# Sixteen gate chunks of a streaming-encoder layer computed as eight 2x2 block products of seven

## The chip, the cores and the metric

The kernel runs on one core of a Trainium2 chip. The metric is the device time of one execution in microseconds (us), the median of several runs. Engines: TensorE (PE in the profile, its weight loads PEld), VectorE (DVE), ScalarE (ACT), GpSimd (POOL) and SyncE (SP), whose queue issues most DMAs. Each runs its own instructions in order and waits on semaphores for the others.

## The reference

One layer of a residual encoder on x of 1024 tokens by 1024 channels, float32. Of its three sub-layers only the first is touched:

```python
h = rms_norm(x, norm_mix_pre)
q, k, v, u, gate_logits = split(h @ w_in)          # 512 columns each, gate_logits 2048
gate_attn, gate_ssm = split(sigmoid(gate_logits + b_gate))
merged = gate_attn * (stick_breaking_attention(q, k, v) @ w_branch_attn) \
       + gate_ssm * (s5_branch(u) @ w_branch_ssm)
x = x + rms_norm(merged @ w_out, norm_mix_post)
```

Cross-attention into 256 memory tokens and a gated MLP with a causal convolution follow. The change concerns the 2048 columns of gate_logits, 1024 tokens by 1024 by 2048, which before are computed as sixteen chunks of 128 columns.

## The kernel before

**Products in three parts.** A float32 operand is split into a high part (a cast to fp32r on ScalarE) and a low part (the difference, on VectorE). `mm3` (L140) makes each product of three matmuls: high by high, high by low, low by high. A step of TensorE is one `mm3` on a 128x128 stationary and a 128x512 moving tile, planned at STEP = 0.70 us.

**The order.** Up to the branches' merge, order is written by a planner. `at(t, go)` (L227) puts a piece of work at a planned time, and `all_events` issues everything sorted by that time, so planned times set only the order in each engine's queue. On the chip an instruction starts when it is first in its queue and its tiles are ready.

**hT.** The normalised input, x times the gain, transposed, lies in SBUF as high and low parts (`hT`, L333, four tiles of 16 KB per partition in pool ha); the rate of each token (the root-mean-square factor) is applied after the products. v and u are projected first (`tokens`, L423), token blocks against w_in.

**Gate chunks.** `gate_job(gi)` (L283) makes a `Job` (L242): load 512 KB of weights (`load`), cast the high part (`high`, ScalarE), subtract for the low part (`low`, L257, VectorE), and for two halves of 512 tokens eight steps over k into a PSUM bank of tag f (two banks). Then ScalarE copies the bank to SBUF (L288) and a DMA stores it in g_d in DRAM. In all 16 chunks x 2 halves x 8 steps. The merge, far behind, loads g_d again (`gate_load`), scales by the token's rate and applies the sigmoid with the bias (`gate_sigmoid`, L1310).

**Where they run.** The gate steps fill TensorE in two stages. Chunks EARLY_SSM (seven) run beside the SSM branch: `fill_to` (L848) lays one step after the other between the planned instructions of eight SSM slots. A slot n is `flip_u` (transpose u), `states` (L727: matmuls, then VectorE rotates by cosT and sinT, scans, and rotates back into rc, L741 to L753), `outputs` (L759: matmuls with Tt and with rc, then GELU on ScalarE). Slots are SLOT = 12.2 us apart, outputs 9.5 us after states. Between them VectorE prepares what later slots need: `tables` (L641, cosT and sinT of two slots), `operators` (L660, W) and `readout` (L672, F1). After two slots `flip_y` transposes y; when the last is done, `y_high` and `y_low` split it and the GLU follows: four `glu_job`s of eight steps on yh and yl. The other nine chunks, EARLY_ATT, run beside the attention, with the q and k projections of the four head pairs (`qk_job`), as a list `fills` into which the attention's groups (scores, transposes, weigh) are spread evenly: scores on TensorE, two sigmoids on ScalarE, a scan on VectorE (L1022), a product on GpSimd (L1028), transposes, high and low parts of the weights (L1049, L1054), and the product with v (L1067). Scores are laid some 20 us ahead of the transposes that use them.

**Buffers.** Raw weights sit in a ring of two (tag ws), parts in a ring of six (tag w), four tiles of 16 KB hold hT. The SSM stage has six PSUM banks of tag m.

The lines around the change:

## Time and profile before

| | before |
|---|---|
| runs | 1655.45, 1655.84, 1657.39 us |
| median | 1655.84 us |
| span of the profiled execution | 1653.9 us |
| HBM read, written in it | 204.0 MB, 67.4 MB |

The span runs from the first to the last instruction of one profiled execution. The page gives no separate time of that execution, so its span stands for it; the median of the runs is 1.9 us more. In the profile L12 is line 12 of the kernel, "out<-in" are names of tiles, and a row of the timeline is start, duration, engine, line, operation, tiles, shape and count, with idle time before it and what ended it in brackets. TensorE's durations overlap those of their neighbours, so its pace is the distance between two starts. The first 54 us project v, the next 47 u, the SSM stage runs to 218.4 us, the GLU to 240.8, the attention to 537.4, and memory keys and values, merge, cross-attention and MLP fill the rest.

### The profile page before, as it was taken

The numbers are of one execution on the slowest core, as the hardware profiler recorded it, in microseconds if no ns is written. First come the engines' busy times: TensorE is split into PE (matmuls) and PEld (weight loads), VectorE is DVE, ScalarE is ACT, GpSimd is POOL, SyncE is SP. The second block draws the span as 40 slices with busy tenths as digits, with TensorE's granted clock in tenths as the row PEclk, the third lists the DMA queues.
The fourth block names the chain that finished last, engine by engine and source line by source line (L and its number), as shares of the span: only waits on it lengthen the run. The fifth ranks groups of instructions, "written<-read, shape, count | busy, mean of one in ns | idle before, by whom it ended". The sixth has DMA issues, their size and how long they took to land.

```text
span 1653.9 us, 22415 instructions
## 1 busy us (share of the span) xinstructions
PE 1633.8 (99%) x8062; PEld 1379.8 (83%) x8062; DVE 1163.6 (70%) x1616; ACT 880.1 (53%) x1459; POOL 202.2 (12%) x296
## 2 busy tenths in 40 slices
PE   9999999999999999999999999999999999999998
PEld 7998887888888988888888888888888888888886
DVE  6778637776866687467655678888887788775473
ACT  5434346676766544344444556656565556654441
POOL 5000002333332000011000000111111111000010
PEclk9999999999999999999999999999999999999999
DMA  9412144232433954464423574677777676688672
GB/s 323 124 46 66 61 144 110 71 102 80 113 99 127 336 190 136 158 211 158 141 69 129 205 271 175 187 210 211 214 195 206 186 203 185 210 311 280 192 237 81
DMA packets 125439, 279.26 MB, mean 169 GB/s; under 512 B 23696, under 2 KB 28304, under 8 KB 125200
## 3 DMA queue, kind: packets, MB, share of 16 engines
q1 hardware_dynamic: 113664, 251.35, 46.1%
q0 software_dynamic: 9360, 18.09, 6.3%
q10 hardware_dynamic: 2304, 8.39, 1.3%
q8 instruction: 63, 1.03, 0.3%
q14 instruction: 48, 0.39, 0.1%
HBM read 203.98 MB, written 67.38 MB: 164 GB/s over the span
## 4 chain that ended last, share of the span: by engine, by line
PE 89%; DVE 6%; DMA 2%; ACT 2%; issue 1%; POOL 0%; SPq 0%; DVEq 0%; POOLq 0%; ACTq 0%
PE ps_p L1921 8%; PE ps_p L1919 8%; PE ps_p L1920 8%; PE ps_f L141 7%; PE ps_f L143 7%; PE ps_f L142 6%; PE ps_d L2190 4%; PE ps_d L2189 4%; PE ps_d L2191 4%; PE ps_m L141 3%; PE ps_m L143 3%; PE ps_m L142 3%; PE ps_o L1067 2%; PE ps_w L1042 2%; PE ps_z L141 1%; PE ps_z L142 1%
## 5 line engine op out<-in xcount | busy, mean ns | idle before, releaser
L141 PE MATMUL ps_f<-hT,wh 128*128 128x512 f32 x384 | 161.3, 420 | 0.0
L143 PE MATMUL ps_f<-hT,wl 128*128 128x512 f32 x384 | 150.8, 393 | 0.0
L142 PE MATMUL ps_f<-hT,wh 128*128 128x512 f32 x384 | 150.6, 392 | 0.0
L1920 PE MATMUL ps_p<-qS,bm 128*128 128x512 f32 (+2 forms) x368 | 140.4, 382 | 1.7 <-DVE qS L1744 1.7
L1919 PE MATMUL ps_p<-qS,bm 128*128 128x512 f32 (+2 forms) x368 | 140.5, 382 | 1.4 <-DVE uu L1937 0.9
L1921 PE MATMUL ps_p<-qS,bm 128*128 128x512 f32 (+2 forms) x368 | 140.5, 382 | 0.0
L147 DVE TENSOR_TENSOR dn<-raw,dn 128x1024 fp32r<-128x1024 f32 x77 | 93.4, 1223 | 63.0 <-ACT dn L146 59.2
L146 ACT CAST dn<-raw 128x1024 fp32r<-128x1024 f32 x77 | 80.5, 1054 | 87.2 <-PE ps_d L2191 36.4
L2189 PE MATMUL ps_d<-dn 128*128 128x512 f32 x308 | 119.8, 389 | 0.0
L2190 PE MATMUL ps_d<-dn 128*128 128x512 f32 x308 | 119.8, 389 | 0.0
L2191 PE MATMUL ps_d<-dn 128*128 128x512 f32 x308 | 119.8, 389 | 0.0
L1028 POOL TENSOR_TENSOR s<-s,s 128x127 f32<-128x127 f32 (+4 forms) x96 | 89.9, 937 | 223.8 <-DVE s L1022 178.6
L1921 PE MATMUL ps_p<-qA,bm 128*128 128x512 f32 (+2 forms) x272 | 105.1, 386 | 0.5 <-DVE bm L1850 0.5
L1919 PE MATMUL ps_p<-qA,bm 128*128 128x512 f32 (+2 forms) x272 | 105.3, 387 | 0.0
L1920 PE MATMUL ps_p<-qA,bm 128*128 128x512 f32 (+2 forms) x272 | 105.0, 386 | 0.0
L1932 ACT COPY uu<-ps_p 128x512 f32<-128x512 f32 (+2 forms) x90 | 51.5, 572 | 90.0 <-PE ps_p L1921 90.0
L1862 POOL DMA_DIRECT2D bm<-in_ffn_up_T x61 | 52.7, 864 | 356.6 <-ACT bm L1861 144.2
L143 PEld LDWEIGHTS ps_f<-hT,wl 128*128 128x128 f32 x384 | 72.1, 188 | 16.3
L1016 ACT ACTIVATE s<-ps_z,rates_x 128x128 f32<-128x128 f32 (+3 forms) x96 | 56.3, 587 | 54.0 <-PE ps_z L1005 47.8
L1919 PEld LDWEIGHTS ps_p<-qS,bm 128*128 128x128 f32 x368 | 69.2, 188 | 15.2 <-ACT uu L1932 2.2
L1920 PEld LDWEIGHTS ps_p<-qS,bm 128*128 128x128 f32 x368 | 69.2, 188 | 15.1 <-DVE qS L1744 2.0
L1921 PEld LDWEIGHTS ps_p<-qS,bm 128*128 128x128 f32 x368 | 69.3, 188 | 13.2
(544 smaller groups left out, 4462.2 us busy)
## 6 DMA issues: line engine op xcount, KB each, us to landing
raw<-sd SPq DMA_DIRECT2D x77, 256.0 KB, 3.5
bm<-in_ffn_up_T POOLq DMA_DIRECT2D x61, 256.0 KB, 5.4
ws<-in_w_in_T SPq DMA_DIRECT2D x24, 512.0 KB, 3.3
ws<-in_xa_wo_N SPq DMA_DIRECT2D x23, 512.0 KB, 4.3
wv<-in_ffn_up_T SPq DMA_DIRECT2D x22, 512.0 KB, 4.0
wg<-in_ffn_up_T SPq DMA_DIRECT2D x22, 512.0 KB, 3.8
dr<-in_ffn_down SPq DMA_DIRECT2D x22, 512.0 KB, 6.4
td<-st SPq DMA_DIRECT2D x44, 256.0 KB, 5.9
```

Source lines behind the costliest of these rows:

```text
L141: T.matmul(acc, sh, mh, start=first, stop=False)
L142: T.matmul(acc, sh, ml, start=False, stop=False)
L143: T.matmul(acc, sl, mh, start=False, stop=last)
L146: C.copy(dh, src)
L147: (lo or V).tensor_tensor(dl, src, f(dh), op=ALU.subtract)
L1028: G.tensor_tensor(s1[:, n0:e], s1[:, n0:e], s2[:, n0 + 1:e + 1], op=ALU.mult)
L1919: T.matmul(acc, bm[:, 0, ks], q[:, 0, k, cs], start=alone and k == 0, stop=False, skip_group_check=True)
L1920: T.matmul(acc, bm[:, 0, ks], q[:, 1, k, cs], start=False, stop=False, skip_group_check=True)
L1921: T.matmul(acc, bm[:, 1, ks], q[:, 0, k, cs], start=False, stop=k == 3, skip_group_check=True)
L2189: T.matmul(acc[i], v[:, 0, 0, sl], v[:, 0, 1], start=first, stop=False, skip_group_check=True)
L2190: T.matmul(acc[i], v[:, 0, 0, sl], v[:, 1, 1], start=False, stop=False, skip_group_check=True)
L2191: T.matmul(acc[i], v[:, 1, 0, sl], v[:, 0, 1], start=False, stop=last, skip_group_check=True)
```

## The change

Two neighbouring gate chunks m = 0, 1 (columns), two halves of the 1024 input channels and two halves of the tokens form a 2x2 by 2x2 block product, which is made of seven products instead of eight. The class `Product` is one of the seven for one of the eight pairs: four steps over k on a sum (or difference) of two weight blocks (`total`, or one block alone for products 2 and 5) and a moving tile. For products 3 and 4 the moving tile is a quarter of hT, for the others a quad: `quad(n, ...)` loads two quarters of x transposed (a new input x_Q), adds or subtracts them, multiplies by the gain, and splits the sum into high and low parts in the one tile of a new pool psl. That pool holds first the raw x tiles of the beginning, then quads 7, 6, 2, 5 and 1 in turn, each for all pairs that need it.

A product's result goes to one or two of the pair's four quadrants in g_d. The first that arrives is stored; a later one is added by a DMA that GpSimd issues with accumulate. Some pairs of products (4 and 7, and 3 and 6 for pairs 2 and 3) stay in one PSUM bank and leave it once. Where a product counts negative for one quadrant, the quadrant is kept negated, and the sigmoid takes a scale of -1 (`sign_of`).

Beside the SSM now run products 4 and 7 of all pairs, 3 of pairs 0 to 3 and 6 of all, 28 in all, with sums and low parts on GpSimd (`lower=G`). Beside the attention run 2, 5, 3 of pairs 4 to 7, and 1, with sums and low parts on VectorE. To make room in SBUF, tables are built in place, W and F1 have two buffers for three and four, q and k tiles share rings of three, s1 tiles are cut to size, oT has one buffer. `readout` 2 and 3 and `operators` 2 move from the u projection into the SSM slots, SLOT becomes 13.6 and outputs lie 10.5 us after states. One PSUM bank of tag m becomes tag g for products.

```diff
--- before.py
+++ after.py
+    FACTOR = {1: ((0, 0), (1, 1)), 2: ((0, 0),), 3: ((1, 0), (1, 1)), 4: ((0, 1), (0, 0)), 5: ((1, 1),),
+              6: ((0, 0), (1, 0)), 7: ((0, 1), (1, 1))}
+    QUAD = {1: ((0, 0), (1, 1)), 2: ((1, 0), (1, 1)), 5: ((0, 0), (0, 1)), 6: ((1, 0), (0, 0)), 7: ((0, 1), (1, 1))}
+    LESS = (3, 4, 6, 7)
+    GIVES = {1: {(0, 0): 1, (1, 1): 1}, 2: {(1, 0): 1, (1, 1): -1}, 3: {(0, 1): 1, (1, 1): 1}, 4: {(0, 0): 1, (1, 0): 1},
+             5: {(0, 0): -1, (0, 1): 1}, 6: {(1, 1): 1}, 7: {(0, 0): 1}}
+    CHAINED = {4: (0, 0), 3: (1, 1)}
+    def sign_of(gi, th):
+        return -1 if (gi % 2 if gi >= 8 else (gi + th) % 2) else 1
+    def first_in(pair, th, m):
+        if m == 0:
+            return (4,) if th else (7,)
+        if th == 0:
+            return (3,) if pair < 4 else (5,)
+        return (3,) if pair < 2 else (6,)
+    quads = {}
+    def quad(n, tag, t, parts=(0.0, 5.0), ahead=8.0):
+        (ta, ka), (tb, kb) = QUAD[n]
+        minus = n in LESS
+        rows, cs = {}, [slice(512 * j, 512 * j + 512) for j in range(2)]
+        def column(k, hh, j):
+            i = 4 * k + 2 * hh + j
+            return gcol[:, 0, i:i + 1]
+        def load(hh):
+            kw = {"bufs": WS} if tag == "ws" else {}
+            rows[hh] = [wpool.tile([P, 1024], F32, tag=tag, name="xq", **kw) for _ in range(2)]
+            for r, (th, kh) in zip(rows[hh], QUAD[n]):
+                dma(r, a["x_Q"][th, kh][:, hh * 1024:(hh + 1) * 1024])
+        def scaled(hh):
+            x = rows[hh][1]
+            for j in range(2):
+                C.activation(x[:, cs[j]], x[:, cs[j]], AF.Identity, bias=zcol, scale=column(kb, hh, j))
+        def total(hh):
+            xa, x = rows[hh]
+            if minus:
+                V.tensor_tensor(x, xa, x, op=ALU.subtract)
+                return
+            for j in range(2):
+                V.scalar_tensor_tensor(x[:, cs[j]], xa[:, cs[j]], column(ka, hh, j), x[:, cs[j]],
+                                       op0=ALU.mult, op1=ALU.add)
+        def high(hh):
+            if not hh:
+                quads[n] = psl.tile([P, 2, 4, 512], F32R, tag="slot", name="S")
+            for j in range(2):
+                dst, src = quads[n][:, 0, 2 * hh + j], rows[hh][1][:, cs[j]]
+                if minus:
+                    C.activation(dst, src, AF.Identity, bias=zcol, scale=column(ka, hh, j))
+                else:
+                    C.copy(dst, src)
+        def low(hh):
+            for j in range(2):
+                (h_, l_), src = (quads[n][:, m, 2 * hh + j] for m in range(2)), rows[hh][1][:, cs[j]]
+                if minus:
+                    V.scalar_tensor_tensor(l_, src, column(ka, hh, j), f(h_), op0=ALU.mult, op1=ALU.subtract)
+                else:
+                    V.tensor_tensor(l_, src, f(h_), op=ALU.subtract)
+        for hh, d in enumerate(parts):
+            at(t + d - ahead, lambda _, hh=hh: load(hh))
+            if not minus:
+                at(t + d - 2.2, lambda _, hh=hh: scaled(hh))
+            for go, dt_ in ((total, -1.3), (high, 0.0), (low, 1.3)):
+                at(t + d + dt_, lambda _, go=go, hh=hh: go(hh))
+    banks_of = {}
+    class Product:
+        home, tag = None, "f"
+        def __init__(self, pair, n, chain=None, lower=None):
+            self.i, self.n, self.chain, self.lower = pair, n, chain, lower or V
+            into = {}
+            for (th, m), sign in GIVES[n].items():
+                if chain == "begins" and (th, m) == CHAINED[n]:
+                    continue
+                into.setdefault(sign * sign_of(2 * pair + m, th), []).append((th, m, n not in first_in(pair, th, m)))
+            self.into = list(into.items())
+        def load(self, t):
+            self.ws = (wpool.tile([P, 1024], F32, tag="ws", name="ws", bufs=WS) if self.home is None else
+                       self.home.pool.tile([P, 1024], F32, tag="ws", name="ws", bufs=1))
+            for j, (m, k) in enumerate(FACTOR[self.n]):
+                dma(self.ws[:, j * 512:(j + 1) * 512], a["w_in_T"][8 + 2 * self.i + m][:, k * 512:(k + 1) * 512])
+        def total(self, t):
+            if len(FACTOR[self.n]) == 2:
+                self.lower.tensor_tensor(self.ws[:, :512], self.ws[:, :512], self.ws[:, 512:],
+                                op=ALU.subtract if self.n in (3, 4) else ALU.add)
+        def high(self, t):
+            self.bm = wpool.tile([P, 2, 512], F32R, tag="w", name="bm")
+            C.copy(self.bm[:, 0], self.ws[:, :512])
+        def low(self, t):
+            self.lower.tensor_tensor(self.bm[:, 1], self.ws[:, :512], f(self.bm[:, 0]), op=ALU.subtract)
+        def weights(self, t0, load=16.5, add=11.5, hi=9.0, lo=7.0):
+            for dt_, go in ((load, self.load), (add, self.total), (hi, self.high), (lo, self.low)):
+                at(t0 - dt_, go)
+        def step(self, t, k):
+            n = self.n
+            if n in QUAD:
+                mh, ml = (quads[n][:, j, k] for j in range(2))
+            else:
+                q, cols = (0, slice(0, 512)) if n == 3 else (1, slice(512, S))
+                mh, ml = (hT[j][q][:, k, cols] for j in range(2))
+            if k == 0:
+                self.acc = banks_of.pop(self.i) if self.chain == "ends" else ps(self.tag)
+                if self.chain == "begins":
+                    banks_of[self.i] = self.acc
+            wh, wl = (self.bm[:, j, k * P:(k + 1) * P] for j in range(2))
+            for j, (st, mv_) in enumerate(((wh, mh), (wh, ml), (wl, mh))):
+                T.matmul(self.acc, st, mv_, start=self.chain != "ends" and k == 0 and j == 0, stop=k == 3 and j == 2,
+                         skip_group_check=True)
+            if k == 3:
+                self.out(t + STEP + 0.2)
+        def out(self, t):
+            pool, tag, bufs = logs[-1]
+            def put(sign, places):
                 gt = pool.tile([P, 512], F32, tag=tag, name="glog", bufs=bufs)
-                C.copy(gt, acc)
-                dma(g_d[gi][:, sl], gt)
-
-            at(t, put)
-
-        return Job(a["w_in_T"][8 + gi], out)
+                if sign < 0:
+                    C.mul(gt, self.acc, -1.0)
+                else:
+                    C.copy(gt, self.acc)
+                for th, m, adds in places:
+                    dst = g_d[2 * self.i + m][:, th * 512:(th + 1) * 512]
+                    if adds:
+                        at(t + 1.5, lambda _, dst=dst: G.dma_start(dst, gt, accum_op=ALU.add))
+                    else:
+                        dma(dst, gt)
+            for x in self.into:
+                at(t, lambda _, x=x: put(*x))
...
-    ra.enter_context(banks(keep="f", m=(512, 6)))
+    ra.enter_context(banks(keep="f", m=(512, 5), g=(512, 1)))
...
-    logs.append((pa, "vt", 1))
+    logs.append((pa, "vt", 3))
+    xall = psl.tile([P, 4, KT, P], F32, tag="slot", name="xt")
...
-    SLOT = 12.2
+    SLOT = 13.6
...
-    at(u_begin + 33.2, lambda t: readout(t, 2))
-    at(u_begin + 35.4, lambda t: readout(t, 3))
-    at(u_begin + 37.6, lambda t: operators(t, 2))
+    quad(7, "ws", u_begin + 4.0, (0.0, 9.5), 7.0)
...
+    prods = []
+    for q in range(0, 8, 2):
+        prods += [Product(p, 4, "begins", lower=G) for p in (q, q + 1)]
+        prods += [Product(p, 7, "ends", lower=G) for p in (q, q + 1)]
+    prods += [Product(p, 3, lower=G) for p in (0, 1)]
+    prods += [Product(p, 3, "begins", lower=G) for p in (2, 3)]
+    prods += [Product(p, 6, "ends", lower=G) for p in (2, 3)]
+    prods += [Product(p, 6, lower=G) for p in (0, 1, 4, 5, 6, 7)]
+    tags = itertools.cycle("ffg")
+    for n, j in enumerate(prods):
+        j.home = open_t if n % 3 == 2 else None
+        j.tag = next(tags) if j.chain != "ends" else None
+        for k in range(4):
+            steady.append(lambda t, j=j, k=k: j.step(t, k))
+    first_of = {64 + 4 * n: j for n, j in enumerate(prods)}
...
+                if ns == 64 + 64:
+                    quad(6, "w", clock + 0.6, (0.0, 9.0))
...
-            plan(s0 + 9.5, 1.75, outputs, n)
+            plan(s0 + 10.5, 1.75, outputs, n)
...
-                if 1 <= n <= 4:
-                    at(s0 + 6.4, lambda t, n=n: readout(t, n + 3))
+                if n:
+                    at(s0 + 6.8, lambda t, n=n: readout(t, n + 1))
...
-            if n == 0:
-                at(s0 + 8.5, lambda t: operators(t, 3))
-            if n == 1:
-                at(s0 + 8.5, lambda t: tables(t, 3))
+            if n in (0, 2):
+                at(s0 + 8.5, lambda t, n=n: operators(t, 2 + n // 2))
+            if n in (1, 3):
+                at(s0 + 8.5, lambda t, n=n: tables(t, 2 + n // 2))
...
+    quad(2, "w", clock + 9.0, (0.0, 13.0), 8.0)
...
+    fills, phase = [], {n: [Product(p, n) for p in range(8)] for n in (2, 5, 1)}
+    phase[3] = [Product(p, 3) for p in (4, 5, 6, 7)]
+    def fill_pair(js, together=False):
+        seq = [(j, h) for h in range(2) for j in js] if together else [(j, h) for j in js for h in range(2)]
+        fills.extend((j, (h, k)) for j, h in seq for k in range(KT))
+    def fill_products(js):
+        fills.extend((j, (k,)) for j in js for k in range(4))
+    later = [[qk_job(pp, True), qk_job(pp, False)] for pp in range(1, 4)]
+    fill_pair(qk0, True)
+    fill_products(phase[2][:3])
+    fill_pair(later[0])
+    fill_products(phase[2][3:])
+    fill_pair(later[1])
+    fill_products(phase[5][:3])
+    fill_pair(later[2])
+    fill_products(phase[5][3:])
+    fill_products(phase[3])
+    fill_products(phase[1])
...
+        elif isinstance(job, Product):
+            job.weights(t0, 13.0, 7.0, *((2.6, 1.3) if job is phase[3][1] else (5.0, 3.8)))
+            t1 = ended[phase[2 if job.n == 5 else 5][-1]]
+            if job is phase[5][0]:
+                quad(5, "w", t1 + 11.0, (0.0, 17.5))
+            elif job is phase[1][0]:
+                quad(1, "w", t1 + 0.8, (0.0, 3.0), 11.5)
...
-        C.activation(gates[d, h][br], gates[d, h][br], AF.Sigmoid, bias=bgate[:, gi:gi + 1])
+        C.activation(gates[d, h][br], gates[d, h][br], AF.Sigmoid, bias=bgate[:, gi:gi + 1],
+                     scale=float(sign_of(gi, h)))
```

94 lines of the change are left out of this document (43 added, 51 removed).

## Prediction

> **What bounds the kernel now.** I read the page's first and fourth parts, then the windows by stage, then who TensorE waited for.
>
> ```profile
> span 1653.9 us, 22415 instructions
> PE 1633.8 (99%) x8062; PEld 1379.8 (83%) x8062; DVE 1163.6 (70%) x1616; ACT 880.1 (53%) x1459; POOL 202.2 (12%) x296
> PE 89%; DVE 6%; DMA 2%; ACT 2%; issue 1%; POOL 0%; SPq 0%; DVEq 0%; POOLq 0%; ACTq 0%
> ...
> 101.50:218.40 116.90, 116.23 (x676) 101.52 (x676) 87.76 (x147) 49.51 (x64) 1.19 (x9) 1.00 0.22 69
> 240.80:537.40 296.60, 294.89 (x1629) 250.75 (x1628) 209.66 (x279) 200.56 (x415) 92.19 (x159) 1.00 0.35 102
> 480.00:520.00 40.00, 40.00 (x223) 34.12 (x223) 26.47 (x36) 27.66 (x59) 14.12 (x24) 1.00 0.38 112
> ...
> PE ps_w L1042 <- DVE wtl L1054: 1.2, 2, 0.7
> PE ps_m L767 <- DVE rc L753: 0.7, 1, 0.7
> PE ps_o L1067 <- DVE wtl L1054: 0.6, 1, 0.6
> ```
>
> TensorE is the bound: busy 99% of the span, 89% of the chain of waits, clock 1.00. The window rows give us, then busy PE, PEld, DVE, ACT, POOL, the clock, the DMA share and GB/s. Gate work lies in two stages: beside the SSM (the first window, 112 steps of three matmuls) and beside the attention (the second, 144 gate steps and 128 of q and k). In both TensorE lacks under 2 us, and the three waits shown, 2.5 us together, are the ones on VectorE there. So a matmul taken out shortens the span by its pitch, as long as VectorE, with 71% of the attention and 75% of the SSM stage, keeps up. It has the next-fullest queue, and the change fills it.
>
> **What goes.** Sixteen chunks of two halves and eight k are 256 steps, 768 matmuls. Eight pairs, seven products, four k make 224 steps, 672 matmuls. The SSM stage keeps 112 steps, the attention goes from 272 to 240. Matmuls overlap, so their price is the pitch from start to start:
>
> ```profile
> 218.44 0.40 PE L141 MATMUL ps_f<-yh,wh 128*128 128x512 f32 x1
> 240.61 0.39 PE L143 MATMUL ps_f<-yh,wl 128*128 128x512 f32 x1
> 240.84 0.39 PE L141 MATMUL ps_f<-hT,wh 128*128 128x512 f32 x1
> 255.58 0.39 PE L143 MATMUL ps_f<-hT,wl 128*128 128x512 f32 x1
> ```
>
> Between the last two rows lie 65 pitches: 14.74/65 = 0.227 us on hT. 96 matmuls fewer are **-21.8 us**.
>
> **Slower operand.** The first two rows are the GLU: 95 pitches in 22.17 us, 0.2334. Its moving tiles lie in a late pool, hT's in an early one. The five quad sums go to a new pool behind hT, so 5 x 8 x 12 = 480 matmuls may run at the GLU's pitch: 480 x 0.0065 = **+3.1 us**, or 0 if they run like hT. I take 3.1: like yh they are new tiles outside hT's pool. The Trainium skill, SBUF — State Buffer, section Who interferes with whom, has TensorE waiting on nobody at SBUF; by that this term would be 0 and the sum 3.1 lower, but these rows show two pitches.
>
> **SSM stage.** Here each of eight slots is a chain: states on TensorE, rotation and scan on VectorE (L741 to L753), outputs on TensorE, which need rc. Slots come every 13.6 us by the new plan (12.2 before).
>
> ```profile
> 118.57 0.69 DVE L668 TENSOR_TENSOR W<-pr,X 128x512 f32<-128x512 f32 x1
> 120.50 0.69 DVE L668 TENSOR_TENSOR W<-pr,X 128x512 f32<-128x512 f32 x1
> ...
> 123.20 0.69 DVE L741 TENSOR_TENSOR bp<-ps_m,cosT 128x512 f32<-128x512 f32 x1 [0.69 <-PE ps_m L732]
> 125.33 0.69 DVE L744 TENSOR_TENSOR bp<-bp,bt 128x512 f32<-128x512 f32 x1
> ...
> 130.18 0.28 DVE L691 TENSOR_TENSOR ktt<-ps_m,dm 128x128 f32<-128x128 f32 x1
> ...
> 131.51 0.68 DVE L678 TENSOR_TENSOR F<-pr,Y 128x512 f32<-128x512 f32 x1
> ...
> 133.44 2.38 DVE L652 TENSOR_TENSOR x<-x,turns 128x8 f32<-128x8 f32 x7
> ...
> 137.72 0.68 DVE L741 TENSOR_TENSOR bp<-ps_m,cosT 128x512 f32<-128x512 f32 x1
> ```
>
> From start to start: a chain is 130.18 - 123.20 = 7.0 us (the first 2.1 of it read PSUM), a readout 1.9, a table 4.3, an operator pair of two halves 3.9. This slot was full already, its successor started late (no idle before 137.72), and TensorE paid the 0.7 us of L767. The change takes seven lows off VectorE and moves two readouts and one operator pair from the u projection into the slots. Slot 1 and slot 3 then hold 7.0 + 0.2 + 1.9 + 4.3 = 13.4 us, slot 2 12.8, slot 0 11.1, slots 4 and 5 with half of quad 6 each 7.0 + 1.9 + 2.4 = 11.3, slot 6 8.9. Alone this fits 13.6. But 28 products bring 56 sums of 512 columns to GpSimd (the halves' sum and the low part of each), by the plan's lead times 44 of them in slots 0 to 6, six in each, and the two engines shut each other out:
>
> ```profile
> 296.07 1.09 POOL L1028 TENSOR_TENSOR s<-s,s 128x511 f32<-128x511 f32 x1 [1.74 <-DVE s L1022]
> ...
> 296.21 2.03 DVE L259 TENSOR_TENSOR wl<-ws,wh 128x1024 fp32r<-128x1024 f32 x1 [0.29 <-ACT wh L255]
> ...
> 350.45 2.07 POOL L1028 TENSOR_TENSOR s<-s,s 128x511 f32<-128x511 f32 x1 [2.24 <-DVE s L1022]
> ...
> L259 DVE TENSOR_TENSOR wl<-ws,wh x28: 684/1218/2089, 100.8 to 514.8; 128x1024 fp32r<-128x1024 f32 x24, 128x512 fp32r<-128x512 f32 x4
> ```
>
> A VectorE low that meets a GpSimd product takes 2.03 us for a median of 1.22, 0.81 longer; a GpSimd product that comes second takes 2.07 for 1.09. One sum of six falls on the PSUM part of the chain, five meet the rest. In full that is 5 x 0.81 = 4.1 us a slot: slots 1, 2 and 3 come to 17.5, 16.9 and 17.5, slots 4 and 5 to 15.4, over 13.6 by 3.9 + 3.3 + 3.9 + 1.8 + 1.8 = 14.7 us. The outputs are planned 1 us later than before, and the chain, longer by two meetings, uses that up, so a late chain is a stall of TensorE; queued behind it are all further product steps. If half of the sums fall into gaps it is 2.0 a slot, and 1.8 + 1.2 + 1.8 = 4.8 us. I take the middle, **+10 us**, with 4.8 and 14.7 for the range.
>
> **The seam to the GLU.** By the plan's own times the last product step now lies before the outputs of slot 7; before, 14 steps came after them. They covered this:
>
> ```profile
> 206.40 0.39 PE L767 MATMUL ps_m<-F,rc 128*128 128x128 f32 x2
> 206.82 0.60 ACT L772 ACTIVATE y<-ps_m 128x512 f32<-128x512 f32 x1 [0.21 <-PE ps_m L767]
> 208.02 1.03 PE L783 MATMUL ps_m<-ident,y 128*128 128x128 f32 x8
> 212.52 1.22 DVE L916 TENSOR_TENSOR yl<-U,yh 128x1024 fp32r<-128x1024 f32 x1 [1.77 <-ACT yh L913]
> ```
>
> TensorE waits for the GELU (206.79 to 207.42, 0.7 us with its start), turns y until 1.03 us later, and the last yl is ready 213.74 - 209.05 = 4.7 us after that. The GLU can run three steps of 0.7 before it needs it: 2.6. Together **+3.3 us** (2.6 to 4).
>
> **Attention.** The lows stay on VectorE here.
>
> ```profile
> L1336 DVE TENSOR_TENSOR ml<-mm,mh 128x512 fp32r<-128x512 f32 x16 | 11.0, 689 | 4.8 <-ACT mh L1340 4.8
> L259 DVE TENSOR_TENSOR wl<-ws,wh 128x1024 fp32r<-128x1024 f32 x16 | 21.6, 1348 | 1.1 <-ACT wh L255 1.0
> L288 ACT COPY glog<-ps_f 128x512 f32<-128x512 f32 x18 | 10.6, 589 | 6.4 <-PE ps_f L143 5.9
> L1862 POOL DMA_DIRECT2D bm<-in_ffn_up_T x61 | 52.7, 864 | 356.6 <-ACT bm L1861 144.2 <-DVE uu L1937 136.1 <-DVE t L1826 35.4
> ```
>
> VectorE loses nine lows of 1.35 us (12) and gets 28 lows and 12 sums of half the width (40 x 0.69 = 28) and eight operations for each of quads 5 and 1 (11): 210 + 27 = 237 us in 297 - 22 = 275, 86% for 71%. ScalarE gets 28 copies out for 18, and 28 half casts for nine whole ones, and stays under 85%. GpSimd gets 52 accumulating DMAs at 0.86 us, 45 us on 92, and is half idle; each waits there for ScalarE's copy, and behind it are the products L1028, which run 20 us ahead of their transposes. On average nothing is full. The tightest stretch is product 3 of pairs 4 to 7 with quad 1: 16 steps. TensorE needs 0.68 us a step and its part of the attention, (296.6 - 272 x 0.68)/202 = 0.55, so 19.7 us. VectorE's attention work was 26.5 less two lows in 40 us, 0.6 of the time, and gets denser by a tenth: 12.7 us, with 8 x 0.69 and 5.5 for the quad 23.7, late by 4. Lows are planned 3.8 us ahead. I take **+3 us** for this and the q and k stretches, with 0 and 9 as ends (9 if both quads' 11 us are paid almost whole). The single quad slot is refilled while q and k or product 3 run on other tiles; I count it at nothing, and it is the cover for the quads' own 5.5 us each.
>
> **Smaller edits, queues and DMAs.**
>
> ```profile
> oa_d<-oT SPq DMA_DIRECT2D x16, 128.0 KB, 2.4
> ...
> SPq L289 <- ACT glog L288: 114.9, 26, 10.1
> ...
> 537.40:560.00 22.60, 22.60 (x188) 22.38 (x188) 15.85 (x20) 13.55 (x14) 1.05 (x1) 1.00 0.99 355
> ```
>
> The sign in the sigmoid, tables built in place, W and F with fewer buffers and the s1 tiles cut to size add no instruction, and their next user comes after the last reader in the plan: 0. One oT for two makes ScalarE's copy wait for two DMAs of 2.4 us at each head's end, some 3 us after they are issued: 0 to 1 us seven times on an engine that has 15% left, and I count 0. Loads and stores share SP's queue; it already waits up to 10 us for a copy without TensorE noticing, and the raw tiles (two, three beside the SSM) are free again about when the next load is due: 0. Traffic grows: weights 24 MB for 8, sums 54 x 0.25 MB read and written, quads 10 MB, some 45 MB over two stages with DMA shares of 0.22 and 0.35: hidden. Only the last product's two sums run into the memory stage, whose DMA share is 0.99 at 355 GB/s: 2 x 0.75 MB there are 4 us of DMA time. TensorE was busy throughout, so I take 0, with 4 as the end.
>
> **Sum: -21.8 + 3.1 + 10 + 3.3 + 3 = -2.4 us** on the profiled execution. Its page gives the span, 1653.9; the median of the timed runs is 1.9 higher, which I carry over: 1655.8 - 2.4 = 1653.4.
>
> **Rivals.** (A) GpSimd's sums mostly fall into gaps and the attention absorbs its load: -21.8 + 3.1 + 4.8 + 3.3 + 0 = -10.6, 1645; with hT's pitch for the quads 1642. For it: VectorE sits idle 29 us of the SSM stage. Against: those lie in the late slots. (B) Slower: the lock between VectorE and GpSimd is paid whole in slots 1 to 5 and TensorE waits at L767 for rc: -21.8 + 3.1 + 14.7 + 3.3 + 3 = +2.3, and with the attention's upper end +8.3: 1658 to 1664. It decides from 12.4 us of stalls upward. For it: both pairs of rows above show whole exclusion. The Trainium skill's SBUF page, same section, says just that: a VectorE instruction with two SBUF inputs and a GpSimd instruction that reads SBUF block each other for their whole length; the trace agrees (0.81 us a meeting), and by that rule B is the case. Against: a meeting costs only where VectorE has work waiting. The Trainium skill, TensorE: Matmul & The Clock Gate, Part 1, has the clock halved after an idle window of about 3.4 us and warm again after about as long a busy one; three stalls of 3.9 us would then add up to 3 x 1.7 = 5 us (an estimate from that page). Before shows a clock of 1.00 in every window, so no run here shows it yet. (C) The sums don't get shorter because the accumulating DMAs hold GpSimd and late weights stop TensorE in the attention: each of 24 products late by 1 us would be +24, 1675; the half-idle GpSimd speaks against it.
>
> **How the numbers follow.** My forecast (1648 to 1658) 0.42, A 0.28, B 0.26, C 0.04. A measurement can tell about 0.2%, 3.3 us, from no change. Faster by more than that, under 1652.5: A and 0.17 of the forecast, 0.45. Within: the rest of the forecast but a little, 0.22. Slower, over 1659.1: most of B, C and an edge, 0.33. The range leaves out the ends of A and C: 1641 to 1667.
>
> **What would show it.** Right: TensorE 96 matmuls fewer, each quad matmul at a pitch near 0.233; idle before the outputs' second matmul on rc of 5 to 15 us in slots 2 to 6; VectorE's two-input operations in the SSM stage at 1.5 us instead of 0.7 where a GpSimd sum runs; 3 us of idle at the GLU's first steps; VectorE at 85% in the attention. Wrong: no wait on rc, or waits of TensorE on bm (weights late), on the quad tile, or on ps_f's banks.

## The result and the profile after

The changed kernel takes 1713.82 us (median of four runs, 1710.07 to 1719.53) against 1656.47 beside it: 1.035 times as long, 95% interval 1.033 to 1.037. The forecast was 1653.4 with a range to 1667. The page of after, first and fourth parts:

```profile
span 1708.3 us, 22780 instructions
PE 1640.1 (96%) x7966; PEld 1375.5 (81%) x7966; DVE 1237.2 (72%) x1676; ACT 929.8 (54%) x1563; POOL 331.1 (19%) x406
PE 74%; DVE 9%; DMA 6%; ACT 4%; issue 4%; POOL 2%; SPq 1%; POOLq 0%; DVEq 0%; ACTq 0%
```

The 96 matmuls are gone (7966 for 8062), and yet TensorE is busy 6 us longer: some of its matmuls ran slower. It has also lost the chain of waits to others, 26% for 11%. The windows by stage, after, in the columns that the prediction explains, from the end of the u projection: SSM stage, GLU, attention (to the last product of transposed weights and v), rest.

```profile
103.70:251.80 148.10, 127.79 (x666) 107.85 (x664) 117.05 (x155) 67.29 (x103) 78.76 (x66) 0.91 0.53 167
251.80:277.10 25.30, 23.45 (x98) 17.68 (x96) 15.23 (x21) 17.62 (x24) 0.00 (x0) 1.00 0.55 199
277.10:593.20 316.10, 286.10 (x1533) 237.64 (x1532) 249.74 (x329) 220.39 (x464) 137.99 (x210) 0.98 0.71 180
593.20:1708.30 1115.10, 1102.31 (x5248) 921.96 (x5246) 785.09 (x1021) 571.19 (x895) 83.97 (x97) 1.00 0.61 191
```

Cut at the same places, before took 114.1, 22.2, 296.7 and 1116.6 (its u projection ends at 104.3 us; the prediction's first window began inside it). Its SSM stage and attention:

```profile
104.30:218.40 114.10, 113.43 (x665) 98.76 (x664) 87.26 (x146) 49.51 (x64) 1.19 (x9) 1.00 0.21 68
240.60:537.30 296.70, 294.99 (x1630) 250.84 (x1628) 209.66 (x279) 200.56 (x415) 92.19 (x159) 1.00 0.35 103
```

So the SSM stage lost 34.0 us, the GLU 3.1 and the attention 19.4, where 21.8 less was due; the rest is as it was. Who TensorE waited for in the SSM stage of after (us in total, times, longest):

```profile
PE ps_m L912 <- DVE rc L898: 6.0, 1, 6.0
PE ps_m L911 <- DMA ws<-in_w_in_T: 5.4, 1, 5.4
PE ps_m L876 <- ACT Ug L863: 3.4, 3, 2.6
PE ps_m L911 <- DMA Tt<-ktt: 2.4, 1, 2.4
```

L911 is the outputs' matmul on Tt, L912 the one on rc, L876 the states. L911 reads no weights, so I take its wait of 5.4 us, put down to a load of weights in the same DMA queue, as one for Tt too. With another 2.0 us of this kind, the waits for Tt come to 9.8. TensorE is idle 20.3 us of 148.1 there, and it waits for three things: VectorE's chain, the spread of Tt by DMA, and ScalarE's copy of Ug. The list of waits doesn't say which of them is the cause. In the attention it waits mostly for VectorE's and ScalarE's parts of the transposed weights:

```profile
PE ps_o L1221 <- DVE wtl L1208: 19.5, 17, 2.9
PE ps_o L1221 <- ACT wth L1203: 4.3, 4, 2.1
```

### The profile page after: what moved, and what is told of

Its sections match the earlier page's. It is cut to its first block, busy times and chain, and to the rows that moved or that the text cites. A ratio compares the mean times of both kernels' runs of the same rounds, so it can differ in the third digit from the quotient of the medians.

```text
span 1708.3 us, 22780 instructions
## 1 busy us (share of the span) xinstructions
PE 1640.1 (96%) x7966; PEld 1375.5 (81%) x7966; DVE 1237.2 (72%) x1676; ACT 929.8 (54%) x1563; POOL 331.1 (19%) x406
## 4 chain that ended last, share of the span: by engine, by line
PE 74%; DVE 9%; DMA 6%; ACT 4%; issue 4%; POOL 2%; SPq 1%; POOLq 0%; DVEq 0%; ACTq 0%
PE ps_p L2102 7%; PE ps_p L2100 7%; PE ps_p L2101 7%; PE ps_d L2370 4%; PE ps_d L2371 4%; PE ps_d L2372 4%; PE ps_f L141 3%; PE ps_f L142 3%; PE ps_f L411 3%; PE ps_f L143 3%; PE ps_m L141 2%; PE ps_m L143 2%; PE ps_m L142 2%; DMA ws<-in_w_in_T 2%; PE ps_z L141 1%
## 5 line engine op out<-in xcount | busy, mean ns | idle before, releaser
L1182 POOL TENSOR_TENSOR s<-s,s 128x127 f32<-128x127 f32 (+4 forms) x96 | 100.7, 1057 | 180.1 <-DVE s L1176 126.8
L411 PE MATMUL ps_f<-S,bm 128*128 128x512 f32 x420 | 121.9, 413 | 0.9 <-ACT glog L422 0.8
L2370 PE MATMUL ps_d<-dn 128*128 128x512 f32 x308 | 119.8, 389 | 0.0
L2371 PE MATMUL ps_d<-dn 128*128 128x512 f32 x308 | 119.8, 389 | 0.0
L2372 PE MATMUL ps_d<-dn 128*128 128x512 f32 x308 | 119.8, 389 | 0.0
L411 PEld LDWEIGHTS ps_f<-S,bm 128*128 128x128 f32 x420 | 75.6, 194 | 13.6 <-ACT glog L422 1.2
L210 POOL TENSOR_TENSOR rstd<-rstd,mhalf 128x1 f32<-128x1 f32 x24 | 21.7, 907 | 275.0 <-DVE rstd L208 233.8
L1176 DVE TENSOR_TENSOR_SCAN s<-s,begin 128x128 f32<-128x128 f32 (+1 forms) x64 | 63.7, 997 | 11.9 <-ACT s L1170 11.5
```

What stands on the lines that cost most here:

```text
L411: T.matmul(self.acc, st, mv_, start=self.chain != "ends" and k == 0 and j == 0, stop=k == 3 and j == 2, skip_group_check=True)
L1182: G.tensor_tensor(s1[:, n0:e], s1[:, n0:e], s2[:, n0 + 1:e + 1], op=ALU.mult)
L2370: T.matmul(acc[i], v[:, 0, 0, sl], v[:, 0, 1], start=first, stop=False, skip_group_check=True)
L2371: T.matmul(acc[i], v[:, 0, 0, sl], v[:, 1, 1], start=False, stop=False, skip_group_check=True)
L2372: T.matmul(acc[i], v[:, 1, 0, sl], v[:, 0, 1], start=False, stop=last, skip_group_check=True)
```

## The experiments

Lengths of the stages in the profiled executions, cut as above (us):

| kernel | SSM | attention | span |
|---|---|---|---|
| before | 114.1 | 296.7 | 1653.9 |
| the change | 148.1 | 316.1 | 1708.3 |
| e1 Tt spread by ScalarE's queue | 152.8 | 317.7 | 1717.1 |
| e2 no sums in the SSM stage | 126.5 | 316.1 | 1686.7 |
| e3 both | 124.6 | 315.7 | 1685.9 |
| e4 no sums of x (quads) | 141.1 | 305.7 | 1693.7 |
| e5 no sums, no quads anywhere | 117.4 | 311.1 | 1678.2 |
| e6 no accumulating DMAs | 145.5 | 293.9 | 1688.2 |
| e7 plain stores in their place | 147.9 | 299.5 | 1693.9 |
| e8 no sums of weights in the attention | 146.6 | 317.6 | 1710.4 |
| e9 GpSimd's sums over other tiles | 150.7 | 317.5 | 1714.5 |
| e10 two half output tiles | 147.5 | 317.1 | 1710.1 |
| e11 e5 without accumulating DMAs | 117.4 | 280.5 | 1646.9 |
| e12 powers of one column for these DMAs | 148.1 | 293.5 | 1687.8 |
| e13 e6 without quads | 142.2 | 285.2 | 1673.8 |
| e14 e6 and e8 | 148.4 | 285.7 | 1681.4 |
| e15 SSM sums on VectorE | 147.4 | 315.5 | 1711.9 |

Each experiment was timed once. Where one leaves a stage alone (but for the two accumulating DMAs that start in the SSM stage), the SSM stage repeats between 145.5 and 148.4 and the attention between 315.5 and 317.7, so 3 us in a stage are no reading.

### The SSM stage: queue, lock or room?

Three theories: TensorE's inputs are late because SyncE's queue stands still (Q), because VectorE and GpSimd shut each other out (L), or because VectorE is full anyway (F).

**e1** has the spread issued by ScalarE:

```diff
-            at(now + 1.3 * tau, lambda _, tau=tau: dma(Tt[...], ...))
+            at(now + 1.3 * tau, lambda _, tau=tau: C.dma_start(Tt[...], ...))
```

> The change in the SSM stage came out 33.9 us longer (114.1 to 148.0): waits of TensorE of about 20 us (9.8 of them outputs that wait for Tt, 6.0 for rc), the rest a lower clock after them. Here only the eight DMAs that spread Tt are issued by ScalarE instead of SyncE, whose queue holds weight loads that wait for GpSimd's low parts. Theory Q (the queue: Tt comes late because it stands behind weight loads): the three waits on Tt, 9.8 us, and the clock that they cost, some 7 us, go; the stage takes 129 to 133 us. Theory L (the lock of VectorE and GpSimd makes the chain late; Tt only happened to be the last of two late inputs): the outputs wait for rc instead, the stage stays above 142.

The stage got no shorter, 152.8. TensorE still waited for Tt (10.4 us), and longer than in the change for rc (8.3) and Ug (5.3). Q falls as far as it blames SyncE's queue alone. It is not settled that queues are innocent, since Tt now stood in ScalarE's queue and was late there.

**e2** leaves the sums and low parts of weights out of the SSM stage (a GpSimd memset, which only writes, stands for each low part), **e3** does that and e1.

```diff
...
-            self.lower.tensor_tensor(self.bm[:, 1], self.ws[:, :512], f(self.bm[:, 0]), op=ALU.subtract)
+            if self.lower is G:
+                G.memset(f(self.bm[:, 1]), 0.0)
+                return
+            self.lower.tensor_tensor(self.bm[:, 1], self.ws[:, :512], f(self.bm[:, 0]), op=ALU.subtract)
```

> All sums and low parts of weights on GpSimd in the SSM stage are left out (44 of 56 fall there): the product uses the first block alone, and a GpSimd memset of 512 columns, which reads nothing, stands for the low part. The weight loads still share SyncE's queue with Tt, but their tiles come free earlier. Theory L: VectorE's two-input operations are back at 0.69 us, no wait on rc, the stage at 118 or less. Theory Q gives the same for Tt, since the loads no longer wait for GpSimd; both say 114 to 120. Rival F (VectorE is full by its own work of 13.4 us in a slot of 13.6, without any lock): a wait on rc of 3 us or more stays, the stage at 125 or more. If the clock falls only because of stalls, it is 0.99 or more here.

> Both edits: no sums or low parts on GpSimd in the SSM stage (left out as in the run without sums), and Tt spread by ScalarE's queue. If SyncE's queue alone matters once the sums are gone, this is under the run without sums by the waits on Tt that it keeps; if it holds nothing up then, the two agree within 2 us. Theories Q and L together: stage 112 to 116, all that the change lost there.

21.6 us go in e2 (126.5), 23.5 in e3 (124.6): the sums cost most of what the stage lost. Both runs are still above what Q and L had (118 or less, and 112 to 116). F falls as to rc: no wait on rc is left. One stall remains, at quad 6, of 6.8 us in e2 and 3.9 in e3. In e2 the last spread of Tt stands in SyncE's queue right behind two loads for quad 6:

```profile
173.45 1.04 SPq L319 DMA_DIRECT2D xq<-in_x_Q  x2
174.55 0.52 SPq L843 DMA_DIRECT2D Tt<-ktt  x1
```

The spreads of Tt land after 2.6 us in the median there and after 7.7 at most, and this one's 174.55 + 7.7 is where the stall ends (182.4). In e3 ScalarE's cast of quad 6 waits 2.31 us for the sum of x (its row ends in "2.31 <-DVE xq L329") with the last two spreads of Tt queued behind it.

The same VectorE groups, first in after, then in e2 (busy us, mean ns | idle before):

```profile
L897 DVE TENSOR_TENSOR bt<-bp,sinT 64x508 f32<-64x508 f32 x16 | 15.9, 991 | 0.2
L888 DVE TENSOR_TENSOR bt<-ps_m,sinT 64x512 f32<-64x512 f32 x16 | 11.0, 688 | 0.2
L823 DVE TENSOR_TENSOR F<-F,tq 128x512 f32<-128x512 f32 x6 | 8.0, 1332 | 0.2
```

```profile
L891 DVE TENSOR_TENSOR bt<-ps_m,sinT 64x512 f32<-64x512 f32 x16 | 11.0, 688 | 0.2
L900 DVE TENSOR_TENSOR bt<-bp,sinT 64x508 f32<-64x508 f32 x16 | 10.9, 682 | 0.2
L826 DVE TENSOR_TENSOR F<-F,tq 128x512 f32<-128x512 f32 x6 | 4.2, 693 | 0.2
```

L897 of after is L900 of e2, and L823 is L826. With two SBUF inputs the mean rises from 682 to 991 and from 693 to 1332 ns beside GpSimd's sums; the rotation that reads PSUM (L888, L891 in e2) takes 688 in both. That is what the Trainium skill says, SBUF — State Buffer, section Who interferes with whom: a VectorE instruction with two SBUF inputs contends with a GpSimd instruction that reads SBUF, not with one that only writes it. e2's memsets, which only write, agree: its two-input means are 682 to 693 ns.

**e9** parts the lock from what else the sums hold: GpSimd runs as many, but they read two tiles of hT, so no raw weight tile is held by them.

```diff
...
-            self.lower.tensor_tensor(self.bm[:, 1], self.ws[:, :512], f(self.bm[:, 0]), op=ALU.subtract)
+            if self.lower is G:
+                G.tensor_tensor(self.bm[:, 1], f(hT[0][0][:, 0, :512]), f(hT[1][0][:, 0, :512]), op=ALU.subtract)
+                return
+            self.lower.tensor_tensor(self.bm[:, 1], self.ws[:, :512], f(self.bm[:, 0]), op=ALU.subtract)
```

> It parts the lock from the queues in the SSM stage. GpSimd runs as many sums of 512 columns, at the same places, but over tiles of x that nobody waits for; the sums and low parts of the weights themselves are left out there, so no raw weight tile is held by GpSimd and no load stands behind it. The run without sums took 126.5 us for the stage, the change 148.0. Theory L (VectorE's chain is late because GpSimd's sums shut it out): 142 to 150, with waits on rc, and VectorE's two-input operations beside a sum at 1.5 us or more. Theory H (the raw tiles are held too long and SyncE's queue stands still behind their loads): 124 to 130, with no wait on rc.

150.7: as slow as the change, with waits on rc again (6.6 us). The lock costs these 20 us, and not the raw tiles that the sums hold or the loads that queue behind them. The sums still write the low part that the products read; TensorE's list of waits there shows none on it.

**e15** puts the sums on VectorE:

```diff
-        prods += [Product(p, 4, "begins", lower=G) for p in (q, q + 1)]
+        prods += [Product(p, 4, "begins") for p in (q, q + 1)]
...
```

> The whole change, with the 44 sums and low parts of the SSM stage on VectorE instead of GpSimd: no lock (VectorE's operations at 0.69), but six more operations of 0.69 us a slot on an engine whose work in slots 1 to 3 is 13.4, 12.8 and 13.4 us of 13.6: 17.5, 16.9, 17.5, and 15.4 in slots 4 and 5. Theory L with exclusion paid whole (a meeting costs 0.81 us, an own operation 0.69): 140 to 150, about as on GpSimd. If only the place is wrong: 130 or less.

147.4, the same as on GpSimd. The stage has no room for these operations of 512 columns, wherever they are done: on GpSimd each takes VectorE's time by shutting it out. TensorE's waits lie elsewhere here, 13.7 us of them on Ug, so the equal length alone would not prove one cause; VectorE's busy times below say more.

**e4** and **e5** leave the quads out, with their loads, and the products read hT; e5 leaves out the sums and low parts of weights too (memsets as in e2, in both stages).

```diff
     def quad(n, tag, t, parts=(0.0, 5.0), ahead=8.0):
+        return
...
-            if n in QUAD:
+            if n in quads:
                 mh, ml = (quads[n][:, j, k] for j in range(2))
```

> The five sums of x (quads) are left out, in both stages: products 1, 2, 5, 6, 7 take their moving tile from hT's first-row blocks as products 3 and 4 do, so no quad loads (10 MB), no eight VectorE and eight to twelve ScalarE operations each. Theory Q/L for the SSM stage: quad 7 lies in the u phase, quad 6 in slots 4 and 5; only the waits from 189 to 203 us (8 us and the clock of 0.77 there, some 7 us) go, the stage is 130 to 136. Attention: if VectorE's load makes the transposed weights late (theory V), it loses 11 to 16 us of VectorE work near quads 5 and 1 and the stage falls by about as much, 300 to 306; if accumulating traffic does it (theory D), 313 to 316. The pitch of the products' matmuls, all on hT now, is 0.227 where nothing stalls; if it stays at 0.233 for products 1, 2, 5, 6, 7 the moving tile's place isn't what sets it.

> All sums and low parts of weights and all five sums of x are left out, in both stages; a GpSimd memset of 512 columns stands for each low part, and the products read hT. What remains of the change is its 672 matmuls, the new plan of slots and the accumulating DMAs. This is the gain without its price: SSM stage 116 to 119 (114.1 and the seam), GLU 25.3 as before this run (the change's 3.2 us there don't come from the sums), clock 1.00. Attention, where the change took 316: theory V (VectorE's load makes the transposed weights late, and nothing else does): 275 to 279, the 296.6 of before less 21.8. Theory D (the accumulating DMAs, half of the traffic of a stretch in which the DMA engines are at 0.96 to 1.05 from 477 us on, hold the stage by themselves): 285 to 300.

e4 leaves 141.1 in the SSM stage, above the 130 to 136 expected; e5 117.4, as expected. The windows of that stage in e2, e5, e9 and e15:

```profile
103.70:230.20 126.50, 118.01 (x665) 100.61 (x664) 88.81 (x155) 66.83 (x103) 16.69 (x40) 0.97 0.62 192
```
```profile
103.80:221.20 117.40, 114.97 (x666) 98.47 (x664) 83.90 (x149) 63.66 (x99) 16.55 (x40) 1.00 0.61 188
```
```profile
103.90:254.60 150.70, 127.42 (x663) 108.14 (x662) 125.68 (x155) 67.30 (x103) 81.01 (x68) 0.91 0.52 161
```
```profile
105.40:252.80 147.40, 127.21 (x663) 106.70 (x663) 119.81 (x206) 66.96 (x103) 4.20 (x15) 0.92 0.54 166
```

VectorE is the third of a row's busy times. After and e2 have the same 155 VectorE instructions, and they take 117.05 and 88.81 us: 28.2 us of lock. 51 of the 56 sums fall into the stage as cut here, so 0.55 us each. e15 has these 51 on VectorE, and comes to 119.8, 31.0 over e2 or 0.61 us each. e9's sums cost VectorE more still, 125.68.

### The attention: VectorE's load or the DMAs?

Two theories here. V: VectorE's extra work makes the transposed weights late. D: the accumulating DMAs do. e4 came out as V had it, 305.7 in the attention (300 to 306 expected), but it drops the quads' loads along with their sums, so it doesn't part the two. **e6** leaves these DMAs out, **e7** makes them plain stores from the same queue, **e8** leaves out the sums and low parts of weights (as e2, in the attention).

```diff
-                        at(t + 1.5, lambda _, dst=dst: G.dma_start(dst, gt, accum_op=ALU.add))
+                        pass
```

and in e7

```diff
-                        at(t + 1.5, lambda _, dst=dst: G.dma_start(dst, gt, accum_op=ALU.add))
+                        at(t + 1.5, lambda _, dst=dst: G.dma_start(dst, gt))
```

> The 54 accumulating DMAs are left out (only the first term of each gate block is stored), everything else as in the change. SSM stage: if GpSimd's low parts come late because they queue behind accumulating DMAs that wait for ScalarE's copies (theory P, an in-order queue), the stage falls from 148 to under 130; if the lock alone makes them late (L), it stays above 140. Attention: theory D 296 to 305 (the DMA share from 477 us on falls from about 1.0 to 0.6 or less, and loads land in 3 to 4 us for 6.9); theory V 312 to 316.

> The 54 accumulating DMAs become plain stores, issued by GpSimd at the same places, with the same waits (their sums are left out). It tells the issue and its place in GpSimd's queue from the read and add at the DRAM end. If it is the queue (theory P), it agrees with the change within 4 us in the SSM stage, 144 to 152; if it is traffic (D), attention is half-way to the run without them, 300 to 310, or all the way if the add itself is what is slow.

> Sums and low parts of weights in the attention are left out (a GpSimd memset of 512 columns for each low); quads and accumulating DMAs stay, and the SSM stage is the change's own, 146 to 150. VectorE loses 40 operations, some 28 us of 249. Theory V: attention 283 to 292, the rest being the quads. Theory D: 308 or more, since the waits move to the weights that land late.

V as the only cause falls in e8: 40 VectorE operations fewer (289 for 329, 227.68 us for 249.74) and not a us gained, 317.6. What grew instead is ScalarE's wait for stores of the output tile, 19.2 us for 10.5. (e8's memsets put 22.7 us on GpSimd; TensorE waits 0.8 us for one of them.) e6 gains 22.2 us, e7 16.6. So the reading and adding costs most, not the issue or its place in GpSimd's queue. In the SSM stage e6 takes 145.5, so these DMAs do not make GpSimd's low parts late there.

e5 (no preparation, these DMAs kept) gains only 5, and its 311.1 is above both forecasts, 275 to 279 and 285 to 300. It is also longer than e4, which leaves out less. Attention of e4, e5, e6 and e8:

```profile
270.60:576.40 305.80, 283.44 (x1534) 235.31 (x1532) 236.25 (x310) 211.31 (x448) 136.81 (x210) 0.99 0.68 158
```
```profile
248.00:559.20 311.20, 289.01 (x1534) 240.82 (x1532) 213.68 (x270) 211.28 (x448) 147.89 (x239) 0.96 0.66 156
```
```profile
276.60:570.50 293.90, 279.10 (x1533) 235.50 (x1532) 243.04 (x329) 220.80 (x464) 96.00 (x159) 0.99 0.49 149
```
```profile
275.90:593.50 317.60, 286.83 (x1533) 238.65 (x1532) 227.68 (x289) 220.45 (x464) 150.70 (x239) 0.96 0.72 181
```

TensorE's idle time in e5 is 22.2 us, as in e4 (22.4) and 8 less than in the change (30.0). The rest of the difference is the clock: 0.96 for 0.99, and 5.6 us more busy time for the same matmuls. From 527.5 to 544.4 us e5 runs at a granted clock of 0.50.

The DMA queues in the last 118.5 us of the attention, after (queue, packets, MB, share of 16 engines; then median us to landing):

```profile
q1 hardware_dynamic: 11299, 23.96, 56.9%
q0 software_dynamic: 4032, 7.34, 38.6%
...
g_d<-glog POOLq DMA_DIRECT2D x29, 256.0 KB, 7.2
ws<-in_w_in_T SPq DMA_DIRECT2D x27, 256.0 KB, 6.9
```

29 accumulating DMAs hold 38.6% of the sixteen engines for 7.34 MB, 5.3% a MB; the loads and stores take 2.4% a MB (56.9/23.96). Together they are full. Loads for the memory stage (st, r_kl) fall there as well. The two queues move 31.3 MB, where the last 118.5 us of before's attention moved 13.7. A load of weights lands after 6.9 us; in e6 (its last 110 us) after 4.4. The software queue over the whole attention, after and then e7 (51 DMAs in each):

```profile
q0 software_dynamic: 7200, 13.11, 26.9%
```
```profile
q0 software_dynamic: 4000, 13.11, 11.9%
```

The same bytes take less than half of the engines' time as plain stores.

Late DMAs reach TensorE by more than one way. In after ScalarE waits 10.5 us for stores of the one output tile, VectorE 11.8 for weights to land, and ScalarE 10.3 for VectorE's sums of these:

```profile
ACT oT L1231 <- DMA ol_d<-oT: 10.5, 4, 4.8
ACT bm L389 <- DVE ws L384: 10.3, 5, 3.4
...
DVE ws L384 <- DMA ws<-in_w_in_T: 11.8, 6, 3.6
```

**e10** removes the first of these: two tiles of 256 columns for one of 512.

```diff
-                half[n] = pat.tile([P, 512], F32, tag="oT", name="oT", bufs=1)
...
+            oT = pat.tile([P, 256], F32, tag="oT", name="oT", bufs=2)
+            C.copy(oT, o_ps[:, :256])
```

> The whole change, with the attention's one output tile of 512 columns cut in two of 256 (the same memory), each with stores of its own, so that ScalarE's copy waits for stores issued half a head earlier. In the change ScalarE stood 10.5 us in four waits for such stores, up to 4.8 us each, and the casts of the transposed weights stand behind it. Theory O (accumulating DMAs slow the stores, ScalarE waits for them, and TensorE for ScalarE): attention 304 to 310 for 316. Rival R (the loads that land late at VectorE's sums and the copies behind the accumulating DMAs are as late without it): 313 to 317. SSM stage as in the change, 146 to 150.

317.1: the rival R. The wait moved, in e10's list to:

```profile
ACT glog L422 <- DMA g_d<-glog: 6.9, 3, 4.5
...
DVE ws L384 <- DMA ws<-in_w_in_T: 16.3, 7, 4.1
```

**e12** puts an operation of GpSimd's in the place of each of these DMAs, to tell its time from the DMA engines'.

```diff
-                        at(t + 1.5, lambda _, dst=dst: G.dma_start(dst, gt, accum_op=ALU.add))
+                        at(t + 1.5, lambda _: G.tensor_tensor(spare, gt[:, 0:1], mhalf, op=ALU.pow))
```

> Each of the 54 accumulating DMAs is replaced by a GpSimd power of one column (0.54 to 0.9 us each in the trace, against 0.88 median for the issue), read from the same copy and at the same place in GpSimd's queue; the sums are left out. Without the DMAs and without any stand-in the attention took 293.9, with plain stores 299.5, with accumulating DMAs 316.1. Theory D (DMA engines' time): 292 to 298. Theory G (GpSimd's time and its in-order queue, behind which the score products stand): 308 to 316.

The powers take 0.805 us each, where the issues of the change took 1.02 in the mean, and wait for the same copies:

```profile
L429 POOL TENSOR_TENSOR spare<-glog,mhalf 128x1 f32<-128x1 f32 x54 | 43.5, 805 | 21.9 <-ACT glog L425 15.8 <-ACT glog L423 4.1
```

293.5, as with nothing there (293.9). GpSimd's time costs nothing here; what costs is the DMA engines'.

**e11** is the bare change, **e13** and **e14** leave out the accumulating DMAs with the quads or with the lows (edits as above).

> All sums and low parts of weights, the sums of x and the accumulating DMAs are left out: the 672 matmuls in the change's plan, bare. SSM stage 116 to 118 as without preparation. If the accumulating DMAs and the preparation are all that the attention lost, it takes 274 to 278 (296.6 less 21.8, a little for the one output tile); if it stays above 284, the order of the fill or the fewer buffers cost something by themselves. Without preparation but with these DMAs it took 311.1, without them but with preparation 293.9.

> The accumulating DMAs and the sums of x are left out; sums and low parts of weights stay. Attention between the bare 280.5 and the 293.9 without accumulating DMAs. If the quads are what is left (VectorE's 11 us for quads 5 and 1, paid nearly whole, and their pitch, 2 us): 281 to 284; if the 40 sums and lows on VectorE are: 290 to 293. SSM stage as without quads, 138 to 142.

> The accumulating DMAs and, in the attention, the sums and low parts of weights are left out; the sums of x stay. The counterpart of the run without the quads: if the quads make the remaining 13 us, 290 to 293; if the lows on VectorE do, 281 to 285. If both runs lie near 282, either load alone is carried and only their sum is too much.

```profile
248.40:528.90 280.50, 274.99 (x1533) 233.28 (x1532) 204.01 (x270) 210.82 (x448) 101.92 (x187) 1.00 0.43 125
```

The bare attention (row of e11) takes 280.5, a little over the 274 to 278 expected: 5.5 us idle. Without the DMAs, the quads add 5.2 (e14 over e11) or the lows 4.7 (e13 over e11), and both together 13.4 (e6 over e11). That is the third case of e14's expectation, some 3 us above its figure: most of either load is carried alone, and their sum is not. So V is part of the account: VectorE's lows cost 4.7 us by themselves. And the ceiling is low: with all preparation and all sums left out the span is 1646.9, only 7.0 us under before.

## Why the prediction was wrong

**-21.8 for 96 matmuls, +3.1 for the quads' pitch: right.** The matmuls went, and the quads run slower. Three rows of e2:

```profile
140.25 2.88 PE L414 MATMUL ps_g<-hT,bm 128*128 128x512 f32 x12
142.97 2.97 PE L414 MATMUL ps_f<-S,bm 128*128 128x512 f32 x12
145.77 1.56 PE L414 MATMUL ps_g<-S,bm 128*128 128x512 f32 x6
```

From start to start 12 matmuls on hT take 2.72 us, 0.227 each, and 12 on a quad 2.80, 0.233. In e5, where that product reads hT, they take 2.72 too (142.82 to 145.54), so the pitch goes with the moving tile, which e4's expectation asked. But the bare change (e11) gives back 14.8 of the 21.8: 3.3 in the SSM stage, 4.7 in the GLU and 5.6 in the attention, the rest in pieces outside them. In its GLU the granted clock is 0.94, which makes that 1.6 us longer than the change's.

**Seam to the GLU, +3.3: right in size.** TensorE waits 0.9 us for the GELU, and the GLU takes 3.1 more: 4.0, the upper end. The bare SSM stage is 2.4 us longer still (117.4 less 114.1 and the 0.9); 1.4 us of it are waits for Ug, which the prediction did not have.

**SSM stage, +10 (4.8 to 14.7): the first step that failed.** Over its bare length it lost 30.7 us (148.1 - 117.4). The mechanism was named, two engines that shut each other out, and its full price was almost exact: 4.1 us a slot, 28.7 in seven slots, against 28.2 measured. That is partly luck: the prediction had 42 sums at 0.68 us, and there were 51 at 0.55. Wrong was "If half of the sums fall into gaps" and the middle taken for it: the price was paid whole. Wrong too was the step from a late slot to time, 14.7 us at the full price, where leaving the sums out gained 21.6. Of TensorE's waits 6.0 us were on rc, the sign that it named, and 9.8 on Tt, which it did not have. Two things that it left out:
- Quad 6 was counted as 2.4 us of VectorE in a slot with room. From e2 to e5 the stage falls by 9.1 us, since its loads (e2) and casts (e3) stand in in-order queues ahead of Tt.
- The clock. The matmuls behind a stall run at half the pace. In e2, after the one long wait:

```profile
182.38 0.77 PE L914 MATMUL ps_m<-Tt,Ug 128*128 128x128 f32 x2 [6.75 <-DMA g_d<-glog]
182.94 0.63 PE L915 MATMUL ps_m<-F,rc 128*128 128x128 f32 x2
183.36 0.63 PE L914 MATMUL ps_m<-Tt,Ug 128*128 128x128 f32 x2
...
185.50 0.63 PE L915 MATMUL ps_m<-F,rc 128*128 128x128 f32 x2
185.92 1.03 PE L862 MATMUL ps_m<-ident,U 128*128 128x128 f32 x4
```

A pair takes 0.43 us from start to start here, for 0.22 in the slot before, until 186.6. Busy time is 118.01 for 114.97 in e5; the quads' pitch is 192 x 0.0065 = 1.2 of these 3.0 us, so some 1.8 are the clock's after one wait of 6.75. In after it is 127.79, 12.8 more than bare, 11.6 without the pitch, and the clock of the window is 0.91. A wait of 2.04 us was enough there:

```profile
231.91 0.64 PE L911 MATMUL ps_m<-Tt,Ug 128*128 128x128 f32 x2 [2.04 <-DMA ws<-in_w_glu_T]
232.34 0.64 PE L912 MATMUL ps_m<-F,rc 128*128 128x128 f32 x2
```

Each of the five longest waits of after's SSM stage, 2.0 to 6.0 us, is followed by a stretch at a granted clock of 0.50 (from 122.9, 157.1, 191.2, 204.8 and 232.2 us). It is not so after every such wait: one of 2.1 us in the attention left the clock at 1.00 (313.7 to 325.0). The Trainium skill, TensorE: Matmul & The Clock Gate, Part 1, has half speed after an idle window of about 3.4 us, and about as long until it is over. The slow stretch in e2 is a little longer, 4.2 us, and after's shorter waits do not fit that rule, so the measurement decides. Rival B counted three stalls and up to 5 us by it, and the loss was more than twice that.

**Attention, +3 (0 to 9): the second step that failed,** by its DMA term. Due were 296.7 - 21.8 = 274.9; measured 316.1, 41.2 more: 5.6 in the bare version, 13.4 for quads and lows together, 22.2 for the accumulating DMAs. VectorE's part was mis-sized, since 86% full was read as nearly free. The DMA part was put at nothing: "hidden", from a mean share of 0.35 and from bytes (its own terms, 16 + 27 + 10, add up to 53 MB and not 45). In the change the bytes crowd into the last 118 us, 31.3 MB for 13.7; and a sum's bytes hold the engines more than twice as long as a load's, which no row of before showed. "Raw tiles are free again about when the next load is due: 0" failed with it, as the loads landed 2.5 us later.

**One output tile for two, +0: right in the net, by luck.** ScalarE waited 10.5 us there, which the prediction did not expect, but e10 shows that the time would be lost elsewhere.

**The rivals.** B had the sign and the SSM mechanism, and was still 50 us short. C named the accumulating DMAs and +24 in the attention, near the 22.2, with a chance of 0.04 (in place of the +3 it gives 1674, not 1675); but it had them hold GpSimd, and e12 shows that this costs nothing. "The half-idle GpSimd speaks against it" looked at the wrong resource.

## What to carry to other kernels

A saving on the bound engine is worth what its supply allows: take the preparation (sums, low parts, stores of partial sums) out of the new version first and time the bare matmuls, since here that showed a ceiling of 7 us before any of it was paid. Work moved to GpSimd beside a VectorE chain on SBUF was not moved off VectorE here: 0.55 us of its time a sum, for 0.61 done on VectorE. Price an accumulating DMA by DMA engine time in the stretch where it falls, not by bytes over the stage, and a stall of TensorE with the clock that it loses.

## What the runs showed of the hardware

- An accumulating DMA of 256 KB to DRAM holds the DMA engines for 0.269 x 316.1 x 16 / 51 = 26.7 us of engine time, a plain store from the same queue for 0.119 x 299.5 x 16 / 51 = 11.2.
- The lock is by operands: VectorE's operations on PSUM keep 688 ns beside GpSimd's sums, those on two SBUF tiles rise to a mean of up to 1332.
- The pitch of a 512-column matmul is 0.227 us with the moving tile in hT's pool and 0.233 in the quads' pool; the same product that reads a quad at 0.233 in e2 reads hT at 0.227 in e5. Why is open: no run moved a quad to another place.
- A wait of TensorE of 2.04 us was followed by matmuls at half the pace (pairs at 0.43 us for 0.22). Five waits of 2.0 to 6.0 us in after's SSM stage went with 11.6 us of longer busy time. Not every wait of 2 us has this effect.
